# Nested self-attention on one core: loop-carried waits met at once in a loop's first iteration, and GpSimd's casts of x in 128-column pieces

## The chip, the cores and the metric

The kernel runs on one core of a Trainium2 chip. The metric is the device time of one execution in microseconds (us): 328.47 us in the median of three runs before the change (327.2 to 328.7). The core has a matrix engine (TensorE, PE in the profile), a vector engine (VectorE, DVE), a scalar engine (ScalarE, ACT), GpSimd (POOL) and an engine that here mostly issues DMA transfers (SyncE, SP). Each runs its own queue of instructions in order. They wait for each other by semaphores: counters that an instruction raises when it is done and that others wait to reach a value. PEld is the loading of weights into TensorE, which overlaps PE. A name with a q behind it (PEldq, SPq) is the engine's sequencer, which handles registers, branches, semaphores and the issuing of DMAs.

## The reference

32 sequences of lengths from 64 to 511 in a padded array of 512 rows, 8 heads of 64 columns, so 512 columns in all. Beyond its length a sequence's output is zero.

```python
for b in range(batch):
    seq_len = lengths[b]
    qkv = np.matmul(x[b, :seq_len], w_qkv)
    q, k, v = np.split(qkv, 3, axis=-1)
    ...
    scores = scale * np.matmul(q, k.transpose(0, 2, 1))
    attn = np.exp(scores - scores_max)
    attn = attn / (np.sum(attn, axis=-1, keepdims=True) + 1e-08)
    out_b = np.matmul(attn, v).transpose(1, 0, 2).reshape(seq_len, dim)
    output[b, :seq_len] = out_b
```

## The kernel before

**Loops over sorted pairs.** A head sorts the sequences by length. They are then handled longest first, in pairs. There are twelve loops, one for each padded size N of 512, 448, 384, 352, 320, 288, 256, 224, 192, 160, 128 and 96 rows, and a loop handles the pairs whose longer sequence fits its N. How often each runs is known only from the lengths: here 1, 1, 1, 3, 1, 1, 1, 2, 1, 2, 1 and 1 times, 16 iterations in all. So 12 of 16 iterations are their loop's first.

**Positions.** An iteration handles two positions, j = 0 and j = 1, one sequence each. At a position the core works on several sequences at once, which the code calls steps with short names:

- TensorE forms the scores (L1269) of the present sequence, sums the values weighted by their exponentials (L1517, L1557, L1631), and projects the next sequence to queries, keys and values (L1323, L311, L300; L1210 for a partly filled last tile).
- ScalarE takes the exponentials (L1287) and copies banks of the accumulator memory to SBUF; VectorE shares these copies (L1367, L1386, L1442, L1489), which carry names G0, G1 and so on.
- VectorE turns the sums into output: a reciprocal (L1706, L1671), a multiplication of it by a mask of live rows (L1712, L1680), and the product (L1715, L1693). These output operations are O0, O1 and so on, numbered from the end of a position.
- GpSimd casts x of a later sequence to 16 bits and masks its dead rows: casts() at L1060 calls cast() at L363 once for each tile of 128 rows, a two-input operation on 128x512 elements (L371). It also runs gathered() (L1190), which in loops with partly filled last tiles copies the last columns of two transposed sequences side by side (L1195, L1198).
- SP loads x, transposes the casted x by DMA (XT, L328), and stores the output.

**Waits.** plan_waits() (L41) walks once over all the loops and gives every step the waits it needs. A wait of the kind "pos" is for a step of some positions ago; "posin" and "posold" are for steps from before the loop was entered, "iter" for those that count iterations. Since how often a loop runs isn't known, the value to wait for comes from registers: value_of() (L1935) gives each kind its register and amount, which are set where a loop is entered (L2083 to L2091) and raised at the end of an iteration (L2115 to L2123). Between them stand the branch back (L2125) and the entry branch (L2102); L2030 is a separate wait instruction ahead of a step, issued with its step's own waits by issue() (L2017). All semaphores that a first position waits for start from a "lead", a number of increments given at the start (in the head, on the owner's queue or on SP's for VectorE's) so that waits for positions before the first are met.

A "pos" wait from a loop's first position back to the position before it needs, in the loop's first iteration, the last position of the loop before; the plan makes both cases one wait, so it is there in the first iteration whether or not the code of the loop before makes it needless.

Of the kernel before, what the change touches and what calls it, by code (L numbers as in the profile page):

```python
# [18 lines left out]
P = 128  # L19
# [21 lines left out]
def plan_waits(head, bodies, entries, rare):  # L41
# [22 lines left out]
    def follow(chain):  # L64
# [5 lines left out]
        for at, v in enumerate(chain):  # L70
# [10 lines left out]
            for w, j, k, op in todo:  # L81
# [17 lines left out]
                for wait in waits[w, j, k]:  # L99
# [4 lines left out]
                        or (wait[0] == "pos" and o["b"] == b - wait[2])  # L104
                        or (wait[0] == "iter" and o["b"] // 2 == b // 2 - wait[2])
# [13 lines left out]
                for o in sorted(needs, key=lambda o: -o["order"]):  # L119
# [23 lines left out]
                    else:  # L143
                        wait = ("pos", o["name"], b - o["b"])
# [8 lines left out]
                after = dict(mine)  # L153
# [9 lines left out]
                for r in op.writes:  # L163
                    write[r] = o
                    readers[r] = []
# [11 lines left out]
def kernel(  # L177
# [850 lines left out]
    def position(N, j, at, ring):  # L1028
# [161 lines left out]
        def gathered(b):  # L1190
# [3 lines left out]
            if b:  # L1194
                return nc.gpsimd.tensor_copy(  # L1195
                    out=parts[:, :, 0:3:2, :], in_=got.broadcast_to([P, NC, 2, half])
                )
            return nc.gpsimd.tensor_copy(out=parts[:, :, 1:2, :], in_=got)  # L1198
# [701 lines left out]
    waits, has = plan_waits(head, bodies, entries, rare)  # L1900

# [5 lines left out]
    for key, todo in waits.items():  # L1907
        for wait in todo:
# [3 lines left out]
            least = wait[2] if len(wait) > 2 else wait[0] in ("last", "lead")  # L1912
# [22 lines left out]
    def value_of(v, j, wait):  # L1935
# [24 lines left out]
    fixed = defaultdict(set)  # L1960
    for (v, j, k), todo in waits.items():
        op = op_of(v, j, k)
        for wait in todo:
            base, amount = value_of(v, j or 0, wait)
            if base:
                wanted[op.eng].add((base, amount))
                if base in entered:
                    fixed[v, op.eng].add((base, amount))
                if base == "posold":
                    wanted[op.eng].add(("posin", amount))  # L1970
                    fixed[v - 1, op.eng].add(("posin", amount))
# [72 lines left out]
    with tc.tile_critical():  # L2044
# [17 lines left out]
        for e, eng in EN.items():  # L2062
            regs[e] = {}
            for base, amount in sorted(wanted[e]):
                reg = eng.alloc_register(f"{e}_{base}_{amount}")
# [17 lines left out]
        for v, N in enumerate(LOOPS):  # L2083
            for e, eng in EN.items():
                for base, amount in sorted(fixed[v, e], key=lambda f: (f[0] != "posold", f)):
# [17 lines left out]
            with nc.body(body):  # L2103
# [63 lines left out]
```

## Time and profile before

| | |
|---|---|
| median of three runs | 328.47 us (327.2 to 328.7) |
| span of the profiled execution | 328.5 us (no other time of it is given) |
| mean granted TensorE clock | 0.994 of full speed |
| TensorE busy, 0 to 24 us (head) | 20.26 us |
| TensorE busy, 320 to 328.5 us (tail) | 1.03 us |
| GpSimd's casts L371 | 83 of 128x512, 84.2 us in all |
| GpSimd's gathered copies | 6 of L1195 and 6 of L1198 |

The span runs from the first to the last instruction on the core. A row of a timeline gives start and duration in us, engine, line, operation, output and inputs, shape and count, and in square brackets the idle time before it with what ended that idle time; "issue" there means that the engine waited for nothing that the profile shows, so for its own sequencer. A row by source line gives the count, the shortest, median and longest duration in ns, and the first and last start. In a table of stretches each row has the stretch, its length, then busy time with the count for PE, PEld, DVE, ACT and POOL, the granted clock, the DMA engines' share, and GB/s. A chain row gives start, length and operation of the work that ended last. The waits' rows give who waited for whom: us in total, times, and the longest.

### The profile page before, as it was taken

What the parts mean: (1) busy time and instruction counts of PE and PEld (TensorE: products, weight loads), DVE (VectorE), ACT (ScalarE), POOL (GpSimd) and SP (SyncE); (2) the same over time, 40 slices, a digit from 0 to 9 for tenths busy, and PEclk for the clock granted to TensorE, in tenths of its full rate; (3) what the DMA queues carried; (4) which work ended last, traced back from release to release, by engine and by line L of the source; (5) the groups of instructions that cost most, each with busy time, mean ns of one, the idle gap of its engine ahead of it and who ended that gap; (6) DMA issues with size and microseconds to landing.
All of it is one profiled execution on the core that took longest, in us unless ns stands there. A gap on an engine that the chain in (4) does not pass through costs nothing.

```text
span 328.5 us, 13310 instructions
## 1 busy us (share of the span) xinstructions
PE 311.6 (95%) x5092; PEld 202.3 (62%) x5092; DVE 197.7 (60%) x635; ACT 262.6 (80%) x413; POOL 101.9 (31%) x148
## 2 busy tenths in 40 slices
PE   6899999999999999999999999999998999999980
PEld 4444645555655556556656657667777886777860
DVE  6777567566666646456455465545575565776853
ACT  4379999897878988988978989899867779687761
POOL 6448040324030330330231243043222224435320
PEclk9999999999999999999999999999999999999997
DMA  6984749395858999696676766857459857966651
GB/s 217 382 278 80 251 140 327 76 354 153 304 52 298 224 269 258 197 268 224 233 214 224 255 194 205 211 174 242 156 131 227 183 176 164 223 206 177 193 180 66
DMA packets 69449, 68.85 MB, mean 210 GB/s; under 512 B 40720, under 2 KB 40720, under 8 KB 69392
## 3 DMA queue, kind: packets, MB, share of 16 engines
q1 hardware_dynamic: 69344, 68.12, 71.4%
q8 instruction: 33, 0.54, 0.7%
q14 instruction: 24, 0.20, 0.2%
q10 hardware_dynamic: 48, 0.00, 0.0%
HBM read 25.17 MB, written 33.55 MB: 179 GB/s over the span
## 4 chain that ended last, share of the span: by engine, by line
PE 84%; DVE 5%; DMA 3%; issue 2%; ACT 2%; SPq 1%; POOL 1%; DVEq 0%; POOLq 0%; ACTq 0%
PE banks L1323 41%; PE banks L1269 13%; PE banks L1517 12%; PE banks L300 6%; PE banks L311 6%; PE banks L1631 2%; DMA xT<-x 2%; DMA x_nat<-in_x_dram 2%; PE banks L1210 1%; PE banks L1557 1%; DVE out_nat L1715 1%; DVE rcp L1712 1%; DVE out_nat L1693 1%; SPq L328 1%; ACT et L1287 1%
## 5 line engine op out<-in xcount | busy, mean ns | idle before, releaser
L1287 ACT ACTIVATE et<-banks 128x704 f16<-128x704 f32 (+8 forms) x256 | 198.8, 825 | 27.8 <-PE banks L1269 24.7
L371 POOL TENSOR_TENSOR x<-x_nat,mask 128x512 f16<-128x512 f32 x83 | 84.2, 1041 | 184.3 <-DVE mask L1052 174.9
L1323 PE MATMUL banks<-xT,w_r 64*128 64x352 f16 (+9 forms) x1536 | 127.8, 294 | 1.8 <-DMA xT<-x 1.2
L1323 PEld LDWEIGHTS banks<-xT,w_r 64*128 64x128 f16 x1536 | 68.7, 94 | 39.0 <-PE banks L1323 8.5
L1269 PE MATMUL banks<-qz,kT 64*128 64x352 f16 (+11 forms) x624 | 77.5, 294 | 2.6 <-issue 0.7
L1715 DVE TENSOR_TENSOR out_nat<-banks,rcp 128x256 f32<-128x256 f32 (+1 forms) x110 | 53.0, 482 | 3.8
L1367 DVE CAST qz<-banks 128x448 f16<-128x448 f32 (+6 forms) x47 | 26.4, 561 | 45.2 <-PE banks L1323 44.8
L1517 PEld LDWEIGHTS banks<-v_aug,et 128*128 128x128 f16 x1240 | 41.7, 97 | 13.5 <-issue 6.8
L1517 PE MATMUL banks<-v_aug,et 128*128 128x65 f16 x1240 | 47.1, 194 | 0.0
L1323 PE MATMUL banks<-w_r,xT 64*128 64x512 f16 (+1 forms) x368 | 46.6, 372 | 0.3 <-ACT v_aug L1489 0.3
L1269 PEld LDWEIGHTS banks<-qz,kT 64*128 64x128 f16 x624 | 28.1, 93 | 25.9 <-issue 7.1
L1706 DVE RECIPROCAL rcp<-banks 128x4 f32<-128x4 f32 (+1 forms) x112 | 20.3, 181 | 20.7 <-PE banks L1517 7.3
L311 PE MATMUL banks<-w_r,xT 128*128 128x512 f16 x104 | 26.9, 381 | 0.5 <-DVE xT L782 0.5
L1386 DVE CAST v_aug<-banks 128x512 f16<-128x512 f32 x25 | 16.6, 690 | 17.9 <-PE banks L1323 17.9
L1323 PEld LDWEIGHTS banks<-w_r,xT 64*128 64x128 f16 x368 | 17.2, 94 | 14.1 <-PE banks L1323 1.0
L1367 ACT CAST kT<-banks 128x352 f16<-128x352 f32 (+6 forms) x47 | 22.5, 479 | 1.5 <-PE banks L1323 1.5
L300 PE MATMUL banks<-xT,w_r 128*128 128x160 f16 (+3 forms) x256 | 23.0, 243 | 0.5 <-DVE v_aug L1489 0.5
L1367 DVE CAST kT<-banks 128x352 f16<-128x352 f32 (+5 forms) x33 | 17.9, 552 | 7.7 <-PE banks L1323 7.6
L300 PEld LDWEIGHTS banks<-xT,w_r 128*128 128x128 f16 x256 | 16.6, 98 | 5.2 <-DMA xT<-x 0.6
L1367 ACT CAST qz<-banks 128x352 f16<-128x352 f32 (+6 forms) x33 | 15.3, 465 | 3.7 <-PE banks L1323 3.6
L1489 ACT CAST v_aug<-banks 128x512 f16<-128x512 f32 x15 | 8.8, 589 | 9.5 <-PE banks L311 9.5
L1631 PE MATMUL banks<-v_aug,et 64*128 64x65 f16 x624 | 14.2, 190 | 0.6 <-issue 0.6
(116 smaller groups left out, 193.3 us busy)
## 6 DMA issues: line engine op xcount, KB each, us to landing
x_nat<-in_x_dram SPq DMA_DIRECT2D x12, 768.0 KB, 6.4
out_dram<-out_nat SPq DMA_DIRECT2D x12, 768.0 KB, 4.0
x_nat<-in_x_dram SPq DMA_DIRECT2D x14, 512.0 KB, 4.5
out_dram<-zeros SPq DMA_DIRECT2D x12, 512.0 KB, 3.6
out_dram<-out_nat SPq DMA_DIRECT2D x12, 512.0 KB, 4.7
out_dram<-out_nat SPq DMA_DIRECT2D x4, 1024.0 KB, 7.0
x_nat<-in_x_dram SPq DMA_DIRECT2D x3, 1024.0 KB, 5.3
out_dram<-zeros SPq DMA_DIRECT2D x4, 768.0 KB, 4.7
```

The source lines that it names most:

```text
L300: last = nc.tensor.matmul(dst[:, 0:N], w_r[:, c, w0 : w0 + P], xT[:, c, 0:N], start=(c == 0), stop=(c == NC - 1),)
L311: last = nc.tensor.matmul(pv, xT[:, c, t * P : (t + 1) * P], w_r[:, c, 2 * D : 3 * D], start=(c == 0), stop=(c == NC - 1),)
L371: return engine.tensor_tensor(out=x16, in0=x32, in1=live.broadcast_to([P, D]), op=ALU.mult)
L1269: last = nc.tensor.matmul(psc[par][:, x * wide : x * wide + N], kT[r, i, c0 : c0 + P], qz[r, i, 0:N], start=True, stop=True,)
L1287: return nc.scalar.activation(out=et[:, :, x0:x1, 0:N], in_=got.rearrange("p j (x q) -> p j x q", q=wide)[:, :, x0:x1, 0:N], func=AF.Exp, ...
L1323: last = nc.tensor.matmul(to, lhs(rows, c), rhs(rows, c), start=(c == 0 and opens), stop=(c == NC - 1 and not opens),)
L1367: return lambda copy, bank: copy(out=buf[:, ms, 0:M], in_=bank[:, 0 : gm * M].rearrange("p (m q) -> p m q", q=M),)
L1386: return lambda copy, bank: copy(out=v_bufs[o][:, t, :, 0:HD], in_=bank.rearrange("p (h d) -> p h d", d=HD))
L1517: last = nc.tensor.matmul(pav[:, g, qt, :], e_bufs[e][:, c0 + qt * P : c0 + (qt + 1) * P], v_aug[:, kt, h, :], start=(kt == 0 and not (hal ...
L1631: last = nc.tensor.matmul(pavs[own][:, g, qt, :], e_bufs[e][rows, c0 + qt * P : c0 + (qt + 1) * P], (v_bufs[0] if ending else v_aug)[rows, ...
L1706: return nc.vector.reciprocal(out=rcp, in_=pav[:, :, :, HD])
L1715: return nc.vector.tensor_tensor(out=o_t[:, 0:n, h0 * HD : (h0 + heads) * HD].rearrange("p t (g d) -> p g t d", d=HD), in0=pav[:, :, :, 0:HD],
```

## The change

There are three parts.

**Waits.** A "pos" wait that reaches from a loop's body back over its entry becomes a "back" wait. Its register is set at entry, to 1 (met at once) or to the value of the "posin" or "posold" wait on the same step, which it then takes in; at the loop's end it is set to twice the pair's number plus an amount. In the planner a back wait counts as knowledge only on paths that come round the loop, and steps of TensorE that may be skipped no longer add to what later steps know. All computing steps start with the same lead, so that the registers can be shared. These are the lines that do it:

```diff
-                        wait = ("pos", o["name"], b - o["b"])
+                        wait = ("back" if b - o["b"] > (j or 0) else "pos", o["name"], b - o["b"])
...
-                after = dict(mine)
+                after = dict(clock[op.eng] if op.skip < 0 else mine)
...
-                    readers[r] = []
+                    if op.skip >= 0 or op.eng != "PE":
+                        readers[r] = []
...
+    by_dma = {op.name for body in bodies for ops in body for op in ops if op.dma}
+    alike = [name for name in lead if name not in by_dma | rare and lead[name]]
+    for name in alike:
+        lead[name] = max(lead[k] for k in alike)
...
+        if wait[0] == "back":
+            entering = wait[3:] and (wait[3], lead[name] + 1 - wait[4])
+            return "back", (lead[name] + 1 - wait[2] + j, *entering)
...
+                for key in sorted(backs[v, e]):
+                    reg, entering = regs[e][key], key[1][1:]
+                    if not entering:
+                        eng.reg_mov(reg, 1)
+                    elif entering[0] == "posold":
+                        eng.reg_mov(reg, regs[e]["posin", entering[1]])
+                    else:
+                        eng.reg_mul(reg, pair, 2)
+                        eng.reg_add(reg, reg, entering[1])
...
+                    for key in sorted(backs[v, e]):
+                        eng.reg_mul(regs[e][key], pair, 2)
+                        eng.reg_add(regs[e][key], regs[e][key], key[1][0])
```

**GpSimd.** casts() issues four 128x128 operations for a tile instead of one of 128x512; gathered() issues two copies for each of its two.

```diff
             for t in range(n):
-                last = cast(o, t, nc.gpsimd)
+                live = m_bufs[o][:, t : t + 1].broadcast_to([P, P])
+                for c in range(NC):
+                    part = slice(c * P, (c + 1) * P)
+                    last = nc.gpsimd.tensor_tensor(
+                        out=x16_bufs[o][:, t, part], in0=x_bufs[o][:, t, part], in1=live, op=ALU.mult
+                    )
             return last
...
-            if b:
-                return nc.gpsimd.tensor_copy(
-                    out=parts[:, :, 0:3:2, :], in_=got.broadcast_to([P, NC, 2, half])
-                )
-            return nc.gpsimd.tensor_copy(out=parts[:, :, 1:2, :], in_=got)
+            for c in range(0, NC, 2):
+                two = slice(c, c + 2)
+                if b:
+                    last = nc.gpsimd.tensor_copy(
+                        out=parts[:, two, 0:3:2, :], in_=got[:, two].broadcast_to([P, 2, 2, half])
+                    )
+                else:
+                    last = nc.gpsimd.tensor_copy(out=parts[:, two, 1:2, :], in_=got[:, two])
+            return last
```

**An index.** In the packed layout that N = 160 uses, used_by() wraps an index that it clipped before:

```diff
-                mine = {min(k, len(todo) - 1) // across for b in mine for k in (b, b + 1)}
+                mine = {(k % len(todo)) // across for b in mine for k in (b, b + 1)}
```

Where instructions move, on TensorE: the end of an iteration of the 192 loop and the entry of the 160 loop. REGISTER_ALU and ISA rows are register instructions, done_O0 and the like are the semaphores waited for, and numbers behind a name are buffers. Plain register moves and separate wait instructions have no row. Before:

```order
L2115 REGISTER_ALU
L2123 ISA
L2125 COMPARE_AND_BRANCH
L2088 ISA
L2102 COMPARE_AND_BRANCH
L1269 MATMUL banks<-qz_65,kT_69 128x160 [waits done_O0,done_G0,done_G3,done_O2]
L1269 MATMUL banks<-qz_65,kT_69 128x160 x5
L1269 MATMUL banks<-qz_65,kT_69 128x160 [waits done_G0,done_G2,done_O3]
L1269 MATMUL banks<-qz_65,kT_69 128x160 x5
```

The same place after the change, where the line numbers are those of the changed kernel (L1280 is L1269 before):

```order
L2151 REGISTER_ALU
L2159 ISA
L2161 ISA
L2164 COMPARE_AND_BRANCH
L2119 ISA
L2138 COMPARE_AND_BRANCH
L1280 MATMUL banks<-qz_65,kT_69 128x160 [waits done_O0,done_G0,done_G3,done_O2]
L1280 MATMUL banks<-qz_65,kT_69 128x160 x5
L1280 MATMUL banks<-qz_65,kT_69 128x160 [waits done_G0,done_G2,done_O3]
L1280 MATMUL banks<-qz_65,kT_69 128x160 x5
```

One register instruction more (L2161) stands ahead of the branch. The matmuls name the same semaphores; the values that some of them wait for differ.

On GpSimd, casts and gathered copies at the two positions of an iteration of the 448 loop, the first loop with gathered copies. Before:

```order
L371 TENSOR_TENSOR x_74<-x_nat_72,mask_80 128x512 [waits done_LD0,done_XT0,done_M]
L371 TENSOR_TENSOR x_74<-x_nat_72,mask_80 128x512 x3
L1195 COPY last_xT<-xT_76 128x4x2x64
L1198 COPY last_xT<-xT_75 128x4x64 [waits done_XT1]
L2106 UNCONDITIONAL_BRANCH
L371 TENSOR_TENSOR x_73<-x_nat_71,mask_79 128x512 [waits done_LD1,done_M]
L371 TENSOR_TENSOR x_73<-x_nat_71,mask_79 128x512 x3
```

After:

```order
L1067 TENSOR_TENSOR x_74<-x_nat_72,mask_80 128x128 [waits done_LD0,done_XT0,done_M]
L1067 TENSOR_TENSOR x_74<-x_nat_72,mask_80 128x128 x15
L1204 COPY last_xT<-xT_76 128x2x2x64 x2
L1208 COPY last_xT<-xT_75 128x2x64 [waits done_XT1]
L1208 COPY last_xT<-xT_75 128x2x64
L2142 UNCONDITIONAL_BRANCH
L1067 TENSOR_TENSOR x_73<-x_nat_71,mask_79 128x128 [waits done_LD1,done_M]
L1067 TENSOR_TENSOR x_73<-x_nat_71,mask_79 128x128 x15
```

Four casts became sixteen, and each copy became two; the waits stay with the first of each.

More of the change, by code (lines that the diff above doesn't have):

```diff
@@ L104, in follow @@
                         or (wait[0] == "pos" and o["b"] == b - wait[2])
+                        or (wait[0] == "back" and at > chain.index(v) and o["b"] == b - wait[2])
                         or (wait[0] == "iter" and o["b"] // 2 == b // 2 - wait[2])
@@ L1900 @@
     waits, has = plan_waits(head, bodies, entries, rare)
+    for todo in waits.values():
+        for wait in [w for w in todo if w[0] == "back"]:
+            for other in [w for w in todo if w[0] in ("posin", "posold") and w[1] == wait[1]][:1]:
+                todo.remove(other)
+                todo[todo.index(wait)] = (*wait, other[0], other[2])
     def op_of(v, j, k):
@@ L1911 @@
                 continue
-            least = wait[2] if len(wait) > 2 else wait[0] in ("last", "lead")
+            least = max(wait[2::2]) if len(wait) > 2 else wait[0] in ("last", "lead")
             lead[wait[1]] = max(lead[wait[1]], least)
@@ L2063 @@
             regs[e] = {}
[L2064 to L2065 removed]
+            for base, amount in sorted(wanted[e], key=str):
+                reg = eng.alloc_register(f"{e}_{base}_{len(regs[e])}")
                 regs[e][base, amount] = reg
```

10 lines of the change are left out of this document (7 added, 3 removed).

## The prediction

> **What bounds the kernel now.** I read the page's busy times first, then its chain of work that ended last, then a table of three stretches, then the waits.
>
> ```profile
> PE 311.6 (95%) x5092; PEld 202.3 (62%) x5092; DVE 197.7 (60%) x635; ACT 262.6 (80%) x413; POOL 101.9 (31%) x148
> PE 84%; DVE 5%; DMA 3%; issue 2%; ACT 2%; SPq 1%; POOL 1%; DVEq 0%; POOLq 0%; ACTq 0%
> 24.00:320.00 296.00, 290.35 (x4945) 190.79 (x4944) 177.71 (x576) 249.52 (x392) 89.72 (x103) 1.00 0.73 207
> PEld banks L1269 <- issue: 7.1, 17, 0.8
> POOL x L371 <- DVE mask L1052: 174.9, 28, 12.7
> ```
>
> TensorE is the bound: from 24 to 320 us it is busy for 290.35 of 296.00 us, at a granted clock of 1.00. The change takes no matmul away, so it can act on at most 5.65 us there, on the head, and on the tail. The fourth row says what much of the idle time is: 17 times TensorE waited for its own sequencer ("issue"), not for data. The last says that GpSimd sat 174.9 us idle ahead of its casts; it is no bound by its sum.
>
> **Part 1: waits that fall away at a loop's entry.** With these lengths the twelve loops run 1, 1, 1, 3, 1, 1, 1, 2, 1, 2, 1 and 1 times, so 11 iterations are entered from another loop. A wait that is met at once gains only where it ended last. TensorE's loop entries with a stall by an output operation or a bank copy of the previous position are these four (loops of N = 320, 288, 160, 128):
>
> ```profile
> 189.89 0.59 ACT L1489 CAST v_aug<-banks 128x512 f16<-128x512 f32 x1 [1.58 <-PE banks L311]
> 190.43 0.70 ACT L1287 ACTIVATE et<-banks 128x640 f16<-128x640 f32 x1
> 190.53 0.60 PE L1323 MATMUL banks<-w_r,xT 64*128 64x512 f16 x4 [0.25 <-ACT v_aug L1489]
> 212.60 0.56 DVE L1715 TENSOR_TENSOR out_nat<-banks,rcp 128x384 f32<-128x384 f32 x1
> 213.31 0.30 PE L1269 MATMUL banks<-qz,kT 64*128 64x288 f16 x2 [0.20 <-DVE out_nat L1715]
> 288.53 0.42 DVE L1715 TENSOR_TENSOR out_nat<-banks,rcp 128x256 f32<-128x256 f32 x1
> 288.62 0.38 PE L1269 MATMUL banks<-qz,kT 64*128 64x160 f16 x6 [0.36 <-DVEq L2042]
> 309.40 0.59 ACT L1489 CAST v_aug<-banks 128x512 f16<-128x512 f32 x1 [0.26 <-PE banks L311]
> 310.10 0.40 PE L1269 MATMUL banks<-qz,kT 64*128 64x128 f16 x8 [0.25 <-ACT v_aug L1489]
> ```
>
> - 320: the projection starts at 190.53 when the cast of 189.89 + 0.59 = 190.48 is done. Freed, it gains at most its stall of 0.25. The next scores still need the exponentials that end at 190.43 + 0.70 = 191.13, which takes some back: I take **0.2**.
> - 288: the DVE output ends at 213.16, the scores start at 213.31. At most 0.20; I take **0.2**.
> - 160: at most 0.36. One new sequencer instruction stands ahead of it (part 2), so I take **0.3**.
> - 128: the cast ends at 309.99, the scores start at 310.10, but five register and branch instructions stand ahead of them too (part 2). Between 0 and 0.25, I take **0**.
>
> At the other entries the stall names no operation whose wait falls away, so I take 0 there. The two smaller edits to the planner (the clock and the readers of skipped steps) act through these same waits, and the wrapped index of used_by changes no wait of an iteration that runs: 0 for both. Sum of part 1: **0.7**, between 0 and 1.06 (0.25 + 0.20 + 0.36 + 0.25).
>
> **Part 2: what the registers cost.** Every loop's end gets one more register instruction on TensorE's queue (16 executed), eight entries one more move, and the 352, 288 and 192 loops two, one and one more separate wait instructions per iteration (3 x 2 + 1 + 1 = 8 executed). The price is read at the entry of the 256 loop:
>
> ```profile
> L2115 PEldq ALU_OP  x1: 36/36/36, 231.6 to 231.6; - x1
> L2030 PEldq EVENT_SEMAPHORE  x2: 51/51/51, 232.2 to 232.3; - x2
> 231.81 0.36 PE L1557 MATMUL banks<-v_aug,et 64*128 64x65 f16 x12
> 232.37 0.39 PE L1269 MATMUL banks<-qz,kT 64*128 64x256 f16 x4 [0.20 <-issue]
> 275.09 0.34 PE L1269 MATMUL banks<-qz,kT 64*128 64x192 f16 x4 [0.23 <-issue]
> 287.88 0.38 PE L1269 MATMUL banks<-qz,kT 64*128 64x160 f16 x6 [0.23 <-issue]
> L2102 PEldq COMPARE_BRANCH  x1: 77/77/77, 188.9 to 188.9; - x1
> 188.82 1.03 PE L311 MATMUL banks<-w_r,xT 128*128 128x512 f16 x4
> ```
>
> The first row is the loop-end addition, the second the last two waits before the matmul of 232.37. With a combined register step, a branch, another register step and another branch between them, seven instructions start within 231.6 to 232.3: one per 0.7 / 6 = **0.12 us**, though each is busy for some 0.05. The matmuls of 231.81 are over and nothing else is waited for, so an added instruction costs its full 0.12 there. At the entry of the 320 loop it costs nothing: the sequencer has passed the entry branch at 188.9 while TensorE is busy until 189.85 with four matmuls queued ahead. If that cover were gone, it would cost 0.12 too.
>
> By the stalls there are nine boundaries of the first kind (entries of 288, 256, 224, 192, 160, 128, 96 and the back branches of 224 and 160). At 96 the additions cancel; at 160 it is already taken off. Seven times 0.12 is 0.85. The moves (in five of these nine) overlap in part with what the matmul waits for anyway: between 0 and 0.6, I take 0.15. The eight separate waits stand inside an iteration, with matmuls queued ahead: 0, and 1.0 if they aren't covered. Sum: **1.0** lost, between 0 and 2.5.
>
> In the head the semaphores are raised to one common value, with six more increments on SP ahead of its read of the lengths' result:
>
> ```profile
> 3.56 0.47 SPq L664
> ```
>
> This chain row is SP's read, and the input loads follow it. Six increments are worth between 0 (SP waits there for DVE) and 6 x 0.12 = 0.7; since SP waits for DVE, I take **0.1**.
>
> **Part 3: casts and gathers in pieces.** The rows for size:
>
> ```profile
> L371 POOL TENSOR_TENSOR x<-x_nat,mask x83: 1037/1041/1051, 11.5 to 315.5; 128x512 f16<-128x512 f32 x83
> L1997 POOL TENSOR_TENSOR spare<-mask x2: 196/196/197, 318.2 to 322.1; 128x1 f16<-128x1 f32 x2
> L1195 POOL COPY last_xT<-xT x6: 611/612/615, 66.7 to 303.6; 128x512 f16<-128x512 f16 x6
> L1198 POOL COPY last_xT<-xT x6: 402/405/408, 67.2 to 304.1; 128x256 f16<-128x256 f16 x6
> ```
>
> A 128x128 cast isn't in the trace. It costs between 0.20 (the one-column row) and 1.04 (the whole row); on the line between them, 0.196 + 127 x (1.041 - 0.196) / 511 = **0.41 us**, and 0.37 from start to start, since two whole casts take 2.04 (277.63, below) and not 2.08. A tile takes 4 x 0.37 = 1.46 instead of 1.00: 0.46 more, or some 36 us over the 79 tiles that are split. At the ends of the bound a tile takes 0.64 or 4.0 us; I take the line, since the column count is what a piece has less of. That lies in the 174.9 us in which GpSimd idles. The two gathers lose some 0.15 each, by the 0.2 that separates 512 from 256 columns.
>
> What can reach TensorE is VectorE. Its small multiplication by a mask (L1712) reads two SBUF tensors:
>
> ```profile
> 277.63 2.04 POOL L371 TENSOR_TENSOR x<-x_nat,mask 128x512 f16<-128x512 f32 x2 [4.10 <-DVE mask L1052]
> 278.77 0.92 DVE L1712 TENSOR_TENSOR rcp<-rcp,queries 128x4 f32<-128x4 f32 x1
> 280.27 0.31 DVE L1712 TENSOR_TENSOR rcp<-rcp,queries 128x4 f32<-128x4 f32 x1
> 281.05 0.05 issue
> 281.09 0.34 PE banks L1269 x4
> 295.86 2.04 POOL L371 TENSOR_TENSOR x<-x_nat,mask 128x512 f16<-128x512 f32 x2 [2.80 <-DMA x_nat<-in_x_dram]
> 297.74 0.17 DVE L1712 TENSOR_TENSOR rcp<-rcp,queries 128x4 f32<-128x4 f32 x1
> 299.19 0.59 PE banks L1269 x12
> 27.31 4.04 POOL L371 TENSOR_TENSOR x<-x_nat,mask 128x512 f16<-128x512 f32 x4
> 28.68 0.69 DVE L1712 TENSOR_TENSOR rcp<-rcp,v_aug 128x4 f32<-128x4 f32 x1
> ```
>
> It takes 0.17 alone (297.74) and 0.92 at 278.77: it ends at 279.69, just when the cast of 277.63 + 2.04 = 279.67 does. The chain of work that ended last runs through this operation at two places that the pieces touch:
> - In the 192 loop the chain runs through both slow ones (278.77 and 280.27) to the scores of 281.09. A piece holds VectorE for at most 0.41 instead of 0.92, but the pieces last until 277.63 + 8 x 0.37 = 280.6, so the later multiplications meet one too. Gain between 0 and 0.92 - 0.17 + 0.31 - 0.17 = 0.9; TensorE can win back only its own stalls there, so I take **0.35**.
> - In the 160 loop the chain runs through 297.74 to 299.19, where the casts end at 297.90 and now end at 295.86 + 3.0 = 298.8. Two multiplications that were free now meet pieces: between 0 and 2 x (0.41 - 0.17) = 0.5 lost, I take **0.2**.
>
> Does VectorE get in between two pieces? The Trainium skill, "SBUF — State Buffer", section "Who interferes with whom", says that a VectorE instruction with two SBUF inputs contends with a GpSimd one that reads SBUF, and that the second blocks until the first is through. The rows agree: the multiplication of 28.68 ended at 29.37 with the second of four casts (27.31 + 2 x 1.01 = 29.33), and didn't wait for the other two. By the rule a piece blocks for less than a whole cast; if the pair were held over a string of casts, it would be longer (a rival below).
>
> Casts that end later delay the transposing DMA. The tightest place is in the 128 loop:
>
> ```profile
> 309.49 1.20 SPq L328 DMA_TRANSPOSE xT<-x  x1
> 314.30 0.68 PE L300 MATMUL banks<-xT,w_r 128*128 128x96 f16 x12 [0.46 <-DVE v_aug L1489]
> ```
>
> It is issued 4.8 us before its use, and TensorE then waits for DVE instead. Two tiles end 0.93 later, of which some is slack: between 0 and 0.93 lost, I take **0**.
>
> **Sum.** Gains 0.7 + 0.35 = 1.05; losses 1.0 + 0.1 + 0.2 = 1.3. Net +0.25 us on the profiled execution. The profile gives its span, 328.5, and nothing around it; the median of the runs shown is 328.47, so the two stand for the same time. 328.5 + 0.25 is **328.7**.
>
> **Rivals.**
> - *Faster: the stalls go in full.* 1.06 of part 1 and 0.9 of part 3, with all additions hidden: 328.5 - 2.0 = 326.5. For it: the stalls are there. Against it: the "issue" rows at 232.37, 275.09 and 287.88. Chance 0.11.
> - *Slower: the sequencer pays everywhere.* 16 + 8 + 8 = 32 instructions by 0.12 is 3.8, less 1.05: 331.2. It decides where the sequencer isn't ahead of the matmuls, at covered boundaries and inside iterations too. Against it: 188.9 against 189.85. Chance 0.08.
> - *Slower: VectorE is blocked for the whole string.* At 278.77 until 280.6 instead of 279.69, at 297.74 until 298.8: 0.9 + 0.9, with part 2's loss: 328.5 + 1.8 + 1.1 - 0.7 = 330.7. Against it: 28.68. Chance 0.03.
> - *The registers free nothing*, since what TensorE no longer waits for is implied by another wait that stays: part 1 gives 0 and the time is 328.5 + 1.3 - 0.35 = 329.4. It lies within the forecast of no change.
>
> **Chances and range.** No change, 0.78; faster by over 0.5% (1.64 us, about what a measurement of this kernel can tell from no change) 0.11; slower 0.11. The full gains end at 326.5 and the full losses (2.5 + 0.7 + 0.5 + 0.93 - 0) far above 331, but not all terms fall to one side: with half of the gains' 2.0 and no loss the time is 327.5, with half of the losses' 4.6 and half the gains 329.8. A little toward the rivals gives 326.9 to 330.1.
>
> **What would show it.** GpSimd's casts near 0.41 us each and its busy time some 36 us higher; the stalls at 190.53, 213.31 and 288.62 shorter; the "issue" stalls at 232.37, 275.09 and 287.88 longer by 0.12 to 0.24; no L1712 above 0.45 us. I am wrong if the pieces cost twice 0.41 (the transposes then come late), or if the stall-free stretches get longer by themselves.

## The result, and the profile after

The changed kernel takes 330.69 us in the median of 17 runs (329.44 to 332.09), the kernel before 328.58 us in 17 runs beside it (327.2 to 330.88). The ratio is 1.0069 with a 95% interval of 1.0051 to 1.0087: slower by some 2.2 us. The forecast was 328.7 us and no change. The ratios and spans below leave out two executions in a slower state, one of pieces_only (332.09 us) and one of late_240 (517.74 us, at a granted clock of 0.559).

The busy times and the chain that ended last, from the page of the changed kernel, then its rows by source line for the pieces and for the multiplication by a mask (count, shortest, median and longest in ns, first and last start):

```profile
PE 310.4 (94%) x5092; PEld 201.6 (61%) x5092; DVE 196.4 (60%) x635; ACT 262.9 (80%) x413; POOL 137.3 (42%) x394
PE 88%; DMA 4%; DVE 2%; issue 2%; ACT 2%; SPq 1%; POOL 0%; ACTq 0%; POOLq 0%; DVEq 0%
```

```profile
L1067 POOL TENSOR_TENSOR x<-x_nat,mask x312: 392/399/406, 27.6 to 316.0; 128x128 f16<-128x128 f32 x156
```

```profile
L1723 DVE TENSOR_TENSOR rcp<-rcp,queries x54: 161/164/443, 69.8 to 310.2; 128x4 f32<-128x4 f32 x38, 128x6 f32<-128x6 f32 x16
```

GpSimd does what was forecast: 0.40 us for a piece, 35.4 us more busy time in all, and no multiplication by a mask as long as the 0.92 us of before: 0.44 us at most in this row, 0.48 in that of its other form. VectorE fell from 5% to 2% of the chain, DMA rose from 3% to 4%. The places of the prediction, by TensorE's timeline of the changed kernel (start, duration, operation, and in brackets the idle time before and what ended it):

```profile
190.07 1.04 PE L1334 MATMUL banks<-w_r,xT 64*128 64x512 f16 x8
```

```profile
232.47 0.39 PE L1280 MATMUL banks<-qz,kT 64*128 64x256 f16 x4 [0.47 <-issue]
```

```profile
286.60 0.59 PE L1280 MATMUL banks<-qz,kT 64*128 64x160 f16 x12 [0.57 <-issue]
```

```profile
318.21 1.53 PE L302 MATMUL banks<-xT,w_r 128*128 128x96 f16 x32 [1.22 <-DMA xT<-x]
```

At the entry of the 320 loop the projection no longer waits (0.25 us before). At the 256 loop the sequencer's stall grew from 0.20 to 0.47. At the 160 loop the two groups of scores, with 0.23 and 0.36 idle before them, became one group of twelve behind 0.57 of the sequencer's time, so little was gained. At the 288 loop the two stalls of some 0.2 became one of 0.36, and the iteration took 20.94 us, where it had taken 20.93. The last row is new: in the last iteration TensorE waits 1.22 us for the transposing DMA.

The spans of these two profiles, 328.5 and 328.6 us, are no comparison. Each run's time is listed with its span, and in 23 runs of the kernel before the time lay 1.75 to 1.84 us above a span that was 326.4 us in the median. With a span of 328.5 us, the profile that the prediction was made on must have been one of its longest executions (some 330.3 us, an estimate). In the 17 runs of the changed kernel the span is 328.3 us in the median, and 1.94 to 3.11 us lie outside it. So some 1.9 us of the loss lie inside the span, and the rest outside (the 23 runs are those beside the kernels of the next section).

### The profile page after: what moved, and what is told of

Its sections match the earlier page's. It is cut to its first block, busy times and chain, and to the rows that moved or that the text cites. A ratio compares the mean times of both kernels' runs of the same rounds, so it can differ in the third digit from the quotient of the medians.

```text
span 328.6 us, 13636 instructions
## 1 busy us (share of the span) xinstructions
PE 310.4 (94%) x5092; PEld 201.6 (61%) x5092; DVE 196.4 (60%) x635; ACT 262.9 (80%) x413; POOL 137.3 (42%) x394
## 4 chain that ended last, share of the span: by engine, by line
PE 88%; DMA 4%; DVE 2%; issue 2%; ACT 2%; SPq 1%; POOL 0%; ACTq 0%; POOLq 0%; DVEq 0%
PE banks L1334 44%; PE banks L1280 14%; PE banks L1528 12%; PE banks L313 7%; PE banks L302 4%; PE banks L1642 3%; DMA xT<-x 3%; PE banks L1221 1%; PE banks L1568 1%; SPq L330 1%; DMA x_nat<-in_x_dram 1%; PE banks L459 1%; ACT et L1298 1%; PE banks L775 0%; ACT v_aug L1397 0%
## 5 line engine op out<-in xcount | busy, mean ns | idle before, releaser
L1067 POOL TENSOR_TENSOR x<-x_nat,mask 128x128 f16<-128x128 f32 x312 | 112.7, 399 | 149.8 <-DVE mask L1054 148.9
L1280 PE MATMUL banks<-qz,kT 64*128 64x352 f16 (+11 forms) x624 | 77.3, 295 | 3.2 <-issue 1.0
L1280 PEld LDWEIGHTS banks<-qz,kT 64*128 64x128 f16 x624 | 28.0, 94 | 26.4 <-issue 7.3
L313 PEld LDWEIGHTS banks<-w_r,xT 128*128 128x128 f16 x104 | 8.2, 98 | 10.2 <-issue 1.6
```

Of the source, the lines that this page charges most:

```text
L313: last = nc.tensor.matmul(pv, xT[:, c, t * P : (t + 1) * P], w_r[:, c, 2 * D : 3 * D], start=(c == 0), stop=(c == NC - 1),)
L1067: last = nc.gpsimd.tensor_tensor(out=x16_bufs[o][:, t, part], in0=x_bufs[o][:, t, part], in1=live, op=ALU.mult)
L1280: last = nc.tensor.matmul(psc[par][:, x * wide : x * wide + N], kT[r, i, c0 : c0 + P], qz[r, i, 0:N], start=True, stop=True,)
```

## The experiments

All ratios are to the kernel before, run on the same chip beside the kernel. "Outside" is a run's time minus its span: the least, the median and the largest.

```
kernel         ratio   95% interval       span, median  outside
before_again   1.0000  0.9985 to 1.0015   326.1         1.76  1.80  1.84
pieces_only    1.0002  0.9983 to 1.0021   326.4         1.75  1.82  1.84
waits_only     1.0090  1.0061 to 1.0118   328.1         2.04  2.78  3.55
after_again    1.0077  1.0053 to 1.0102   327.9         2.03  2.12  3.65
before_head    1.0078  1.0053 to 1.0102   328.6         1.79  1.95  3.09
before_eight   1.0070  1.0045 to 1.0095   328.8         1.77  1.98  2.01
before_pad     1.0055  1.0034 to 1.0077   327.9         1.83  1.86  1.89
before_110     1.0009  0.9979 to 1.0038   326.6         1.78  1.84  1.87
before_block   1.0031  1.0010 to 1.0053   327.6         1.76  1.79  1.86
after_late     1.0050  1.0032 to 1.0068   327.5         2.04  2.08  3.41
late_110       0.9995  0.9971 to 1.0019   326.0         1.76  1.85  1.93
late_block     1.0058  1.0032 to 1.0084   328.3         1.77  1.84  1.86
late_240       1.0069  1.0043 to 1.0095   328.6         1.79  1.82  1.93
after_block    1.0110  1.0075 to 1.0144   330.3         1.77  1.80  1.85
after_pad      1.0163  1.0136 to 1.0190   331.4         1.76  1.79  1.86
```

**The two halves.** Theory P put the cost with the pieces, theory R with the registers. before_again and after_again are the two kernels unchanged. pieces_only is the kernel before with casts() and gathered() of the change; waits_only is the changed kernel with this in their place:

```diff
         def casts():
             for t in range(n):
-                live = m_bufs[o][:, t : t + 1].broadcast_to([P, P])
...
+                last = cast(o, t, nc.gpsimd)
             return last
```

> The kernel before, unchanged, as the yardstick. Every theory: ratio 1.000 within 0.3%, time near 328.6 us. What it is to show is how far the time of an execution lies above its span: the changed kernel's profiled run took 330.63 us with a span of 328.6 us, so 2.0 us lie outside the span. If that holds for the kernel before too, its usual span is near 326.5 us and the profile that the prediction was made on (span 328.5 us) was one of its longer executions; if the kernel before has no such gap, the change added something outside the span.

> The kernel before with the 128-column casts and the split gathered copies alone; registers, leads and waits as before. Theory P (the pieces cost the 2.1 us: transposes are issued later, their transfers collide and are late in the last loops): ratio 1.005 to 1.008. Theory R (the registers and leads cost it): ratio 0.999 to 1.001. By the prediction's sum it is 0.15 us faster.

> The changed kernel with casts and gathered copies whole again, so waits, registers, leads and the index alone. Theory R: ratio 1.005 to 1.008. Theory P: ratio 0.998 to 1.001. By the prediction's sum (gains of 0.7, losses of 1.1) it is 0.4 us slower, ratio 1.001.

> The changed kernel, unchanged, on the same chip as the two halves: ratio 1.005 to 1.009 by every theory, and the two halves' differences add up to its own if they act apart. Its second profile tells whether the wait of 1.2 us for the transposing DMA in the last loop is there each time (then it is a cost of the change) or not (then it is a matter of one execution).

The pieces cost nothing and gain nothing that this measurement can tell: 1.0002. The waits alone cost as much as the whole change, 1.0090. Theory P falls. The yardstick also settles the span: 326.8 us in its own profile. Against that profile, the start of the register instruction at the end of each loop's iteration (L2115, in the changed kernel L2151) tells where after_again lost: +0.51 us at the end of the 512 loop, hardly any change from there to the end of the 224 loop (+0.53), -0.14 at the end of the 192 iteration, -0.35 after the 160 loop's first iteration, 0.00 before the last iteration, and +0.85 at its end. So there are gains of 0.5 to 1 us in the middle, and a loss ahead of the loops and one in the last iteration. Most of the middle's gain isn't the one that was forecast. In the 192 iteration the kernel before stands still between two matmuls of one group, where no wait is named. This is the profile that the prediction was made on (before_again has the same 0.63 us):

```profile
285.70 0.19 PE L1631 MATMUL banks<-v_aug,et 64*128 64x65 f16 x1 [0.63 <-issue]
```

That stall is gone in after_again, pieces_only and waits_only alike, and also in before_pad, before_110 and before_block below, which have whole casts and the old waits and took 0.74 to 0.76 us less for this iteration.

One gain goes with the pieces and had no term: from the last of these register instructions to the end of the span it takes 6.40 to 6.48 us in the nine profiles with pieces, and 6.83 to 6.93 in the eight without. Why isn't shown.

**Ahead of the loops, and where the code stands.** TensorE's queue has eight more semaphore increments ahead of its first matmul (theory H: these cost time). before_head adds eight to the kernel before, on a semaphore that nobody waits for; after_late takes them from TensorE:

```diff
+        early = tc.alloc_semaphore("early")
+        for _ in range(8):
+            nc.tensor.sem_inc(early, 1)
         pair = nc.alloc_registers("pair")
```

```diff
-            if amount and name in owner:
+            if amount and name in owner and owner[name] != "PE":
...
+            if op.name == "alive0":
+                for name, amount in lead.items():
+                    amount -= name in ahead
+                    if amount and owner.get(name) == "PE":
+                        nc.gpsimd.sem_inc(sems[name], unit(name) * amount)
```

The other idea, theory F (where the code stands costs time), came from the trace of DMA packets, which also has the fetches of instructions. TensorE's code arrives in packets of 16384 bytes (queue q8, 33 in a run of either kernel). In waits_only and after_again such a fetch met the last transposing DMA, and another stood behind the last instruction of the profile, where the kernel before has none. TensorE's built program has 8657 instructions before the change and 8690 after it. So before_pad gives the kernel before 33 instructions that do nothing for the result, and after_pad gives the changed kernel 100, both in the 512 loop (the first two behind a step, as shown, the second four; after_late has nine, so that its code behind stands as in the changed kernel):

```diff
         for name in here["pads"]:
             eng.sem_inc(sems[name], 1)
+        if op.eng == "PE" and v == 0:
+            for _ in range(min(2, here["room"])):
+                eng.sem_inc(here["unused"], 1)
+                here["room"] -= 1
```

> The kernel before with 33 more instructions in TensorE's program and nothing else: increments of a semaphore that nobody waits for, one or two behind each of TensorE's steps of the 512 loop. From the 448 loop on TensorE's code then stands where the changed kernel has it (both programs are 8690 instructions long there, 8657 before). Theory F (the place of the code counts: a 16 KB fetch of TensorE's instructions falls together with the last transposing DMA, whose last part lands some 1.7 us late, and one more fetch is needed when the program ends): the last iteration 0.5 to 1.2 us longer, time minus span 2.0 to 3.6 us instead of 1.8, ratio 1.003 to 1.007. Theory W (what the registers and waits do in the queues costs the time, and where the code stands costs nothing): ratio 0.999 to 1.001, time minus span 1.8 us.

> The changed kernel with 100 such increments in TensorE's 512 loop, so that the last two 16 KB borders of its program are reached 100 instructions earlier. Theory F: no fetch on the way of the last transposing DMA and none behind the program's end, so the last iteration is 1 us shorter than in the changed kernel, time minus span 1.8 to 2.1 us in every run, ratio to the kernel before 1.001 to 1.004. Theory W: ratio 1.007 to 1.010, as the changed kernel or a little worse by the added instructions.

> The kernel before with eight more increments of a semaphore (that nobody waits for) on TensorE's queue ahead of its first matmul, as the common lead adds them in the changed kernel. Theory H (the increments cost 0.15 us each and nothing covers them, which the prediction left out): the first matmul starts at 3.0 to 3.1 us instead of 1.9, the first loop's end comes 0.4 to 0.7 us later, ratio 1.001 to 1.003. Rival: the head is bound by the loads of x and hides them, ratio 1.000.

> The changed kernel with TensorE's nine initial increments issued by GpSimd (behind its clearing of alive, at some 3.2 us, where it waits for VectorE) and nine such increments in the 512 loop so that the code behind stands where it stood. Theory H: TensorE's first matmul starts at 1.8 to 2.0 us, the first loop's end is 0.4 to 0.7 us earlier than in the changed kernel, ratio to the kernel before 1.005 to 1.007. Rival: the same as the changed kernel, 1.007 to 1.008.

TensorE's first matmul, by the timelines of before_again, before_head and after_late:

```profile
1.93 1.89 PE L457 MATMUL banks<-h_ones 128*128 128x256 f16 x8 [1.93 <-POOL h_ones L447]
```

```profile
2.97 0.80 PE L457 MATMUL banks<-h_ones 128*128 128x256 f16 x3 [2.97 <-POOL order_i L488]
```

```profile
1.93 1.89 PE L459 MATMUL banks<-h_ones 128*128 128x256 f16 x8 [1.93 <-POOL h_ones L449]
```

Eight increments put it off by 1.04 us, and 0.44 us of that is left at the end of the 512 loop; without them it is back. The releaser named in the second row is only what came last; TensorE waited for its own queue. The 0.44 us rest on one execution of each kernel: leaving out after_pad, that end comes at 58.40 to 59.01 us in the five profiles with the eight increments, and at 57.66 to 58.55 in the eleven without. But before_head costs 1.0078, over its forecast and far more than 0.44 us. The rest appears in the first iteration of its 160 loop (12.61 us against 11.44) and in its last iteration (6.11 against 5.10). before_pad, whose head is as before, costs 1.0055, and its last iteration took 5.94 us. So theory H is right in its place and too small, and theory F has a case. Its other half failed there: 1.83 to 1.89 us lie outside the span of before_pad, where 2.0 to 3.6 were forecast, and no fetch follows its last instruction. after_pad missed its forecast: its 100 increments, four behind a step, weren't hidden and cost 3.6 us in the 512 loop itself. Its last iteration is 5.35 us against 5.96 in after_again, 0.6 less where 1 was forecast, and 1.76 to 1.86 us lie outside the span in every run, as theory F said.

**Eight hidden instructions, and a whole block.** before_eight and before_block add 8 and 256 increments to the kernel before, at most two behind each projection and bank step; late_block and after_block add 232 and 223 to the changed kernel, with and without TensorE's initial increments moved away, so that the last loop's code stands 256 instructions behind its old place. The edit is the one above with `v in range(6) and op.name[0] in "bg"` for its condition.

> The kernel before with eight such increments in the 512 loop, where they cost nothing, instead of in the head. Theory F: the head is as before, but the code behind stands eight instructions later, as in the run with eight in the head, and the last iteration has the late landing again: ratio 1.003 to 1.006. Theory H alone: ratio 1.000, since the head's increments were the cost.

> A control: the kernel before with 256 more instructions in TensorE's program (two increments of a semaphore that nobody waits for behind each projection and bank step of the loops from 512 to 288), so that every border of 16 KB falls, from the 256 loop on, where it falls in the kernel before. Theory F: what the increments cost by themselves shows at the loops' ends and is under 0.5 us; the last iteration is as before (5.1 us), time minus span 1.8 us, ratio 1.000 to 1.002. If the increments aren't hidden, the loops they stand in show it and the next two are read against this control.

> The changed kernel with both suspected costs taken away: TensorE's initial increments issued by GpSimd, and 232 increments in the loops from 512 to 288, so that the last loop's code stands 256 instructions, one block of 16 KB, behind its place in the kernel before. Theories F and H together: no late landing in the last loop, time minus span 1.8 to 2.1 us, and what the change gains at loops' entries and by the pieces is left: ratio to the kernel before 0.996 to 1.001 (less than the control by 0.3 to 1 us). If the ratio stays over 1.005, the waits themselves cost the time and both theories fall.

> The changed kernel with 223 increments in the same loops and its head as it is. Theories F and H: 0.4 to 0.5 us over the run with the increments issued by GpSimd, ratio 0.998 to 1.003, against 1.007 of the changed kernel.

Eight instructions that are executed once, some 260 us earlier, cost 1.0070, more than forecast. TensorE's timeline in the last iteration of before_again, and then of before_eight:

```profile
315.65 0.35 PE L1269 MATMUL banks<-qz,kT 64*128 64x96 f16 x8 [0.18 <-issue]
315.93 1.53 PE L300 MATMUL banks<-xT,w_r 128*128 128x96 f16 x32
```

```profile
316.68 0.35 PE L1269 MATMUL banks<-qz,kT 64*128 64x96 f16 x8
318.18 1.53 PE L300 MATMUL banks<-xT,w_r 128*128 128x96 f16 x32 [1.15 <-DMA xT<-x]
```

The DMA queues (packets, MB, share of 16 engines' time), of before_again from 315.4 to 316.8 us, behind its last transposition (issued from 312.95 to 314.20, landed at 315.33):

```profile
q1 hardware_dynamic: 136, 0.25, 46.4%
q8 instruction: 1, 0.02, 5.7%
```

And of before_eight from 316.0 to 317.0 us (issued from 313.89 to 315.14):

```profile
q1 hardware_dynamic: 37, 0.08, 19.1%
q8 instruction: 1, 0.02, 6.0%
```

In the kernel before, the fetch starts at 315.42, 0.09 us after the transposition has landed. With eight instructions more the border is reached earlier: the fetch starts 0.41 us after the register instruction at the loop's end instead of 0.68, while the transposition keeps its place (issued until 0.59 us before that instruction, and 0.54 in before_again). The fetch runs from 316.14 to 317.10, 15 of the 16 parts of the transposition land by 316.28, and the last one at 318.13, which is 1.03 us after the fetch ends. Theory H alone would have given 1.000. The last iteration accounts for 1.27 us of before_eight's loss. In the same profile four iterations from the 224 loop to the 128 loop took 0.2 to 0.44 us more each, and no cause is shown for these.

late_block has the forecast last iteration (5.18 us) and nothing extra outside its span (1.77 to 1.86 us), but its ratio is 1.0058. Its control, which has the last iteration of before (5.10), is itself at 1.0031, since its increments cost 1.1 us in the 448 loop (its profile also waits 1.20 us for a transposition in the 224 loop). The first iteration of late_block's 160 loop takes 12.36 us against 11.44. after_block took the same loss there (12.47), and is 1.05 us behind at the end of the 512 loop and another 1.2 us in the 448 loop. The forecasts of these two missed.

**The place, not the number.** before_110, late_110 and late_240 use the loops that hid increments well (`v in (0, 2, 3, 4, 5, 6, 7)`, without 448).

> The kernel before with 110 increments that nobody waits for, in the loops of 512, 384 and 352 (none in the 448 loop, where the control with 256 lost 1.1 us). Theory F, where the place counts and not the number: the fetch in the last loop starts some 2.6 us earlier than in the kernel before and is through before the transposing DMA's last part would land, so the last iteration is 5.1 to 5.4 us, as before, and the ratio is 1.000 to 1.004, less than that of eight increments (1.007). Rival N (each added instruction costs): ratio over 1.007.

> The changed kernel with TensorE's initial increments issued by GpSimd and 86 increments in the loops of 512 and 384, so that the last loop stands 110 instructions behind its place in the kernel before. Theory F: last iteration 5.1 to 5.4 us, time minus span 1.8 to 1.9 us; what the waits and pieces gain at the entries is left if the first iteration of the 160 loop has no late landing: ratio 0.997 to 1.002; with one there 1.003 to 1.006. If it stays at 1.005 or more without late landings, the waits cost time by themselves.

> The same with 216 increments (in the loops from 512 to 288 without 448), so that the last loop stands 16 instructions ahead of its place in the kernel before, a block further on. Theory F: the fetch in the last loop starts after the transposing DMA has landed, last iteration 5.1 us, time minus span 1.8 us; in the 160 loop the fetch comes a little later than in the kernel before. Ratio 0.997 to 1.003.

A hundred and ten instructions cost 1.0009, where eight cost 1.0070: the number isn't it. late_110 is the changed kernel with both costs moved away: 0.9995, against 1.0069 to 1.0077 as it was (its profile is of the longest of its twelve runs, 329.46 us). With the last loop's code 110 instructions behind its old place in both, the kernel before and the changed one are the same within their intervals. TensorE's wait at the same place, of before_110 and of late_110:

```profile
315.17 1.53 PE L300 MATMUL banks<-xT,w_r 128*128 128x96 f16 x32 [0.56 <-DMA xT<-x]
```

```profile
317.17 1.53 PE L302 MATMUL banks<-xT,w_r 128*128 128x96 f16 x32 [0.21 <-DMA xT<-x]
```

The fetch of before_110 ran from 312.75 to 313.71, inside the transposition (issued from 311.67 to 312.91), and all 16 parts landed together at 315.12, 2.2 us after the issue instead of 1.13. That is more than forecast for that spot (5.79 us for the iteration; late_110's 5.46 is over its forecast too). It is hidden in part, and the run gained 0.75 us in the 192 iteration. late_240 is a miss: it has no late part in the last loop and nothing extra outside the span, and yet 1.0069. Its profile loses 0.6 us in the 320 iteration and 0.6 in the last. In the first of these TensorE stands still for 1.02 us ahead of the matmul of 200.81 (L1221), with nothing named but its own sequencer, and a fetch of its code had ended at 199.45. In the 17 profiles, from 24 us on and over 2 us behind any loop's end, there are ten such stalls of over 0.25 us with nothing named but the sequencer, the 0.63 us of the kernel before among them. Each ended 1.23 to 1.66 us behind the end of one of TensorE's own fetches. So where the code stands can cost time in a second way: TensorE seems to wait for the code itself. That is inferred from these times alone. The loss in late_240's last iteration stays open.

**All transpositions of the 17 profiles.** With 74 of them in each, 1258 in all, the 16th part landed over 0.5 us behind the 15th in 105. In 98 of the 105 a fetch of 16 KB ran between the end of the issue (less 0.3 us) and the landing of the 15th part. The late part came 1.06 us after that fetch ended, in the median (0.86 to 1.19). 438 transpositions had such a fetch beside them, so a meeting isn't always late; of the 820 others, 7 were. Sometimes all 16 parts are late together: in the profile of the changed kernel the last transposition was issued from 313.72 to 314.97, a fetch ran from 314.98 to 316.75, and the parts landed from 318.03 to 318.17.

Whether a fetch meets the last transposition separates the 17 profiles by its landing. In nine a fetch ran between the end of its issue (less 0.3 us) and its landing: it landed 2.06 to 3.20 us after its issue, and the last iteration took 5.46 to 6.46 us. In the other eight it landed after 1.13 to 1.33 us, and the iteration took 5.10 to 5.66 us.

Most late parts cost nothing, since TensorE needs them later. At three places TensorE was seen to wait for them: the last iteration, the first of the 224 loop, and the first of the 160 loop, here in after_late:

```profile
293.01 1.20 PE L302 MATMUL banks<-xT,w_r 128*128 128x160 f16 x15 [1.66 <-DMA xT<-x]
```

The fetch there ended at 291.77 and the wait 1.13 us later. That iteration took 12.0 to 12.9 us in five of the profiles (after, after_late, before_head, late_block, after_block), and 11.4 in the two of the kernel before. The 224 loop's place is in the profile that the prediction was made on:

```profile
254.48 0.56 PE L1323 MATMUL banks<-xT,w_r 64*128 64x224 f16 x8 [1.24 <-DMA xT<-x]
```

The late part landed at 254.34, 1.04 us after a fetch ended. That iteration took 15.10 us there and 14.01 in before_again, which is part of why that execution was a long one.

Outside the span, the profiles of after_again and waits_only have a fetch behind their last instruction: after_again's ended at 327.1 us, and this is its queue from there to 331 us.

```profile
q8 instruction: 1, 0.02, 1.9%
```

It ran from 328.99 to 330.18 us, and 2.86 us lie outside that run's span. The profile of the changed kernel itself has no such fetch and 2.03 us outside. Neither profile of the kernel before has one, and 1.8 us lie outside before_again's span. What the other 0.25 us are isn't shown.

## Why the prediction was wrong

- **"What bounds the kernel now"**, and part 3, held in the main. Pieces cost 0.40 us (0.41 forecast; 78 tiles were split, the text counted 79), casts lie in idle time, VectorE isn't held over a string of pieces, and the forecast gain of 0.15 is within what pieces_only can't tell from zero. The gain in the 192 iteration isn't shown to be the forecast one. It measured 0.66 us in after_again and 0.97 in pieces_only, but 0.63 of each is the stall at L1631, which has no part in the forecast.
- **Part 1 gave less than half.** The stalls that it named at the 320, 288 and 160 loops are gone, but what TensorE waited for next took much of it back. Against before_again, after_again gained 0.11 us in the 320 iteration (0.2 forecast), nothing in the 288 iteration (0.2), and 0.21 in the first of the 160 loop (0.3).
- **Part 2 failed, in the price of an instruction.** It priced each added instruction at 0.12 us of queue time where nothing covers it, and at 0 where TensorE has matmuls queued. The queue's price was about right: the stalls at five loop borders (entries of 256, 192 and 128, back branches of 224 and 160) grew by 0.22 to 0.35 us in after_again, 1.35 in all, not all of it the sequencer's by the rows; the term was 1.0. But an instruction also takes a place in the code. 33 more of them, or eight, move the point at which TensorE's next 16 KB are fetched, and in the last loop the fetch then meets a transposition that TensorE needs at once. That cost 0.86 us in after_again and 1.36 us in the first profile of the changed kernel, over the 5.10 us that the iteration takes in the kernel before, and it is the largest single part of the loss inside the span. The sum had no term for it. "The sequencer pays everywhere" (331.2 us) came near the time by luck: its mechanism isn't the one seen.
- **The head was mis-sized.** The text counted six increments on SP and took 0.1. Eight on TensorE's own queue were left out: 1.04 us at the first matmul, some 0.44 us at the end of the 512 loop.
- **"The two stand for the same time" was wrong.** The time is 1.8 us above the span before, and 1.94 to 3.65 after. What happens behind the last instruction wasn't in the sum at all, and the profile taken for a usual one was 2 us longer than that.

Together, against before_again's profile: the changed kernel's own profile lost 0.5 us by the end of the 512 loop, gained 0.6 up to the end of the 192 iteration, lost 0.6 in the 160 loop's first iteration, 0.4 in the two iterations behind it and 1.4 in the last, gained 0.5 at the end of the kernel and lost 0.3 outside the span: 2.1 us. after_again lost 0.5, gained 0.9 up to the 160 loop's first iteration, lost 0.4 and then 0.9 in the last iteration, gained 0.5 at the end and lost 1.0 outside: 1.4 us. How often each late part occurs can't be told, since few executions have a trace: two of the kernel before, two of the changed one, and one of each other kernel.

late_110 shows it from the other side: with the head's increments and the code's place changed, and every wait and piece kept, the loss is gone. It isn't faster than the kernel before either (0.9971 to 1.0019), so no version here beats both. But late_block and late_240 changed the same two things and kept 0.58% and 0.69%, so a place without losses was met by trial, not by a rule that the forecasts had.

The Trainium skill, "Runtime: NRT & Kernel Launch", section "Instruction fetch mechanics", says that an engine's sequencer fetches its program in blocks of 16 KiB, 256 instructions, by a DMA queue of its own, and that the cost of this is mostly hidden. The packets of q8 agree on the size. Here it isn't always hidden: in the last loop TensorE waited 0.67 to 1.22 us in the two profiles of the changed kernel, not for its own code but for the transposition that the fetch met, and the 1.02 us of late_240 look like a wait for the code.

What stays open: which of the 16 DMA engines carries a packet isn't in the trace, so that the fetch and the late part share one is inferred from the 1.06 us and not seen. What late_240 loses besides that 1.02 us, why the kernel's end is shorter with the pieces, and the last 0.25 us outside the span are open too.

## What to carry to other kernels

An instruction added to a long program can cost more than its slot, since it moves the later fetches of code: here eight cost 0.70% and 110 cost 0.09%. Where a change of a few instructions moves the time by 0.5% at a place it doesn't touch, compare the times of instruction fetches with the transfers that are needed at once, and repeat it with the same number of idle instructions in the kernel before. Compare profiles only of executions whose times are known, and keep what lies outside the span as a term of its own.

## What the hardware showed that was not expected

- Eight increments in TensorE's 512 loop, hidden there, lengthened the kernel by 0.70% (0.45 to 0.95), and 110 by 0.09% (-0.21 to 0.38).
- A transposition that meets a 16 KB fetch can have one of its 16 parts land 1.06 us after the fetch's end (0.86 to 1.19), 1.4 to 2.1 us behind the other 15, or have all 16 land late.
- Increments on TensorE's queue ahead of its first matmul took 0.13 us each (1.04 us for eight).
- TensorE stood still ten times for 0.36 to 1.02 us inside an iteration with no wait named, and each time went on 1.23 to 1.66 us behind the end of a fetch of its own code.
